# Eight hand-overs in a transformer block kernel: order of the last FFN up products, places and order of the first FFN down tiles, output weights, first values, conv weights, last splits

## The chip, the cores and the metric

The kernel runs on one core of one Trainium2 chip. The metric is the device time of one execution in microseconds (us); lower is better. Times below are of one profiled execution, unless they are called a median of runs.

## The reference, cut to what matters

One block (DEPTH = 1) on a sequence of 1024 rows of 1024 channels, in float32:

```
h = adaLN(rmsnorm(x))
q, k, v, B, C, X, gA, gB = split(h @ w_in)
A   = stick_breaking_attention(q, k, v)        # 16 heads of 64, strictly causal
Bv  = B * causal_dwconv3(C * X)                # short gated convolution
m   = sigmoid(gA) * (A @ w_branch_a) + sigmoid(gB) * (Bv @ w_branch_b)
x   = x + gate1 * (m @ w_out)
h2  = adaLN(rmsnorm(x))
out = x + gate2 * ((silu(h2 @ w_ffn_gate) * (h2 @ w_ffn_up)) @ w_ffn_down)
```

The attention takes, per query block of 128, a sigmoid of the scores, a running product from the diagonal backwards over the keys, and a product with v. In the kernel the running product is a scan on VectorE, and differences of neighbouring v stand in for the product's last factor.

## The kernel before, in words

Every float32 product is done in three: each operand is split into a high half (`whi`, `ath`, `ya[0]`, `rh`: a copy on ScalarE, rounded to the matmul's format) and a low half (`wlo`, `atl`, `ya[1]`, `rl`: the difference, on VectorE), and TensorE adds high x high, high x low and low x high into one PSUM bank. So each weight tile goes: load into a `raw` tile by SyncE's queue, copy on ScalarE, difference on VectorE, matmul. Tiles come from rings: `bufs` of a tag says how many there are, and a new tile waits until the last reader of the tile that had its place has finished.

The stages that the change touches, in order of time:

- *Attention with fillers* (from about 595 to 990 us). `attention()` walks over steps (head, query block of 128): scores `z` (L913, L914), sigmoid on ScalarE into `pt` (L915), scan on VectorE (L923), transposes `tr` (L936), their split `ath`/`atl` (L939, L940), and the product `o` with the values `vt` (L951, L952). `att_load(h)` loads a head's keys, queries and values, `att_dv(h, e)` forms half e of its value differences from the loads `va`, `vb`. Between these, `fillers()` gives TensorE other products: first those of the conv gate with the weights w_cg (L1012 to L1014), later those of branch B. Program order decides TensorE's order here, and the scan's engine follows it; `tc.issue_after(x)` says that what is inside is to be scheduled behind instruction x.
- *Branch A* (about 995 to 1076). The attention output is loaded into `yr` and split into `ya` (L1160 to L1165), then products (m, n) run over m = 0..7 (output tile) and n = 0, 1 (half of the rows) with weights w_a: 24 matmuls each, in the order (0,0), (1,0), (0,1), (1,1), (2,0), (2,1), (3,0) up to (7,1). The result is multiplied by the gate `sgi` (L1184), added to `mb` (L1185) and split into `big` (L1189 on ScalarE, L1190 on VectorE). The bank of a product is one of two. Each weight tile m is a `raw` of 512 KB from the ring `gw` of two (`g_raw`, L505) and four halves. Beside them, `mods_last()` makes the last adaLN sums on VectorE (`ad`, `msum`, L637) and `preload_wo()` loads and splits the first w_out weights w_o (j = 0, 1, 2; L1142 to L1150), called ahead of m = 6. The number behind a name (raw_10551) is its place in the program.
- *Output projection* (from 1076). `ch` is the half of the columns; per row tile i a product with w_o (L1340 to L1342), the gate (`tm`), the residual into `x1`, a store of `x1` and, in the second half, the second norm (`xn`, L1367) and its transposes (L1245).
- *FFN gate and up* as seven-product Strassen steps (`strassen`, products of 12 matmuls at L131 to L133, sums of halves `c` on VectorE at L136, copies of a bank at L1494), ending at about 1594, then *FFN down* (L1590 to L1592) with tiles `f` of the hidden values, which went through memory (`d_f`), and the weights w_d (`wd`).

What sets the order around the change: the five engines and the DMA queues of SyncE, ScalarE and GpSimd each do their instructions in the program's scheduled order, and wait for each other by semaphores.

Of the kernel before, what the change touches and what calls it, by code (L numbers as in the profile page):

```python
# [9 lines left out]
F32 = mybir.dt.float32  # L10
# [7 lines left out]
P = 128  # L18
# [12 lines left out]
def block_kernel(tc, x, x_t, cols, ada_1, ada_2, ada_row, w_q, w_kv, w_cg, w_a, w_b, w_o, w_g, w_u, w_d, out):  # L31
# [94 lines left out]
    def half_prod(ps, w, fh, fl, onto=False):  # L126

        wh = w[0].rearrange("p (k m) -> p k m", k=4)
        wl = w[1].rearrange("p (k m) -> p k m", k=4)
        for k in range(4):  # L130
            nc.tensor.matmul(ps, wh[:, k, :], fh[:, k, :], start=(k == 0 and not onto), stop=False, skip_group_check=onto)  # L131
            nc.tensor.matmul(ps, wh[:, k, :], fl[:, k, :], start=False, stop=False, skip_group_check=onto)  # L132
            nc.tensor.matmul(ps, wl[:, k, :], fh[:, k, :], start=False, stop=(k == 3), skip_group_check=onto)  # L133

# [757 lines left out]
    lastz = [None]  # L892
    lastld = [None]
    npt = [0]
    ats = {}
# [30 lines left out]
    def att_trans(h, i):  # L926
        pt, off = ptof.pop((h, i)), D - (i + 1) * P
        for b0 in range(0, i + 1, 4):
            nb = min(4, i + 1 - b0)
            key = (h, i // 2, b0 // 4)  # L930
            if key not in ats:
                ats[key] = (at_tile("ath"), at_tile("atl")) if ats else first_at
            th, tl = ats[key]
            tr = pps.tile([P, 512], F32, tag="tr", bufs=NTR, name=nm("tr"))
            for j in range(nb):
                nc.tensor.transpose(tr[:, j * P:(j + 1) * P], pt[:, off + (b0 + j) * P:off + (b0 + j + 1) * P], ident)  # L936
            c0 = (i % 2) * P
            src = tr[:, :nb * P].rearrange("p (j t) -> p j t", t=P)
            nc.scalar.activation(th[:, :nb, c0:c0 + P], src, AF.Copy)  # L939
            nc.vector.tensor_tensor(out=tl[:, :nb, c0:c0 + P], in0=src, in1=th[:, :nb, c0:c0 + P].bitcast(F32),  # L940
                                    op=ALU.subtract)
            yield F_T * nb
# [24 lines left out]
    def attention():  # L967

        steps = [(h, i) for h in range(H) for i in (LAST if h == H - 1 else ORDER)]
        for s in range(len(steps) + DAV):  # L970
            flush[0] = s >= len(steps)
            if s < len(steps):
                h, i = steps[s]
                if s % 8 == (0 if h else 3) and h + 1 < H:
                    with tc.issue_after(lastld[0].ins):
                        att_load(h + 1)
                with tc.issue_after(lastz[0].ins) if s else ExitStack():
                    if s in (1, 2):
# [37 lines left out]
    def fillers():  # L1016
        cb_w = {}
        for m, n in [(m + d, n) for m in range(0, KT, 2) for n in range(2) for d in range(2)]:
            if n == 0:
                with tc.issue_after(lastld[0].ins) if m > 1 else ExitStack():  # L1020
                    cb_w[m] = load_ch(w_cg[0, m])
# [13 lines left out]
            nc.sync.dma_start(d_yb[0][n][:, m, :], yh.bitcast(F32))  # L1035
            nc.sync.dma_start(d_yb[1][n][:, m, :], yl.bitcast(F32))
            yield 0.65 * KQ
# [44 lines left out]
    with tc.high_priority():  # L1082
        att_load(0)
        for j in range(HEAD):
            next(fl)
            if j == 1:
                vl = load_vlast(0)
                turn_vlast(0, vl)
                load_v(0, 1)
                load_v(0, 0)  # L1090
                for e in range(2):
                    nc.sync.dma_start((hh, hl)[e][1][:, :4].bitcast(F32), d_h[e])
# [63 lines left out]
    with tc.high_priority():  # L1156
        for n in range(2):
            for k in range(KT):
# [4 lines left out]
                h_, l_ = ya2[:, 0], ya2[:, 1]  # L1163
                nc.scalar.activation(h_, yr, AF.Copy)
                tt(nc.vector, l_, yr, h_.bitcast(F32), ALU.subtract)  # L1165
# [108 lines left out]
    def prod(ps, w, q, onto=False):  # L1274
        half_prod(ps, w, rh[q], rl[q], onto)

# [27 lines left out]
    for ch in range(2):  # L1304
# [21 lines left out]
        for i in (0, 4, 1, 2, 3, 5, 6, 7) if ch else range(8):  # L1326
# [16 lines left out]
            if last:  # L1343
# [4 lines left out]
                pq[2] = product(s00b, 1)  # L1348
            tm = dp.tile([P, 512], F32, tag="tm", bufs=1, name=nm("tm"))
            nc.vector.tensor_tensor(out=tm, in0=ps, in1=g1b[:, cs], op=ALU.mult)  # L1350
            if ch == 0:
                nc.vector.tensor_tensor(out=tm, in0=tm, in1=xi, op=ALU.add)
# [45 lines left out]
    rh[4], rh[5], rl[4], rl[5] = th[:, 4:8], th[:, 0:4], tl[:, 4:8], tl[:, 0:4]  # L1398
    for q in (6, 3):
        rh[q] = ep.tile([P, 4, 512], F32R, name=f"rh{q}")  # L1400
        rl[q] = ep.tile([P, 4, 512], F32R, name=f"rl{q}")
# [69 lines left out]
    def strassen(j, e, src, done=lambda q, c: None):  # L1471
# [11 lines left out]
        else:  # L1483
# [75 lines left out]
    vt = [e2.tile([P, 512], F32, name=f"vt{t}") for t in range(4)]  # L1559
    f0 = e2.tile([P, 2, 512], F32R, tag="f", bufs=6, name=nm("f"))  # L1560
    wd = [bigp.tile([P, 4, 1024], F32, tag="big", bufs=4, name=nm("wd")) for n in range(4)]
    wd = [w_[:, n, :] for w_ in wd for n in range(4)] + [e2.tile([P, 1024], F32, name=nm("wdx")) for n in range(2 * NJ - 16)]
    def get_f(q, j):
        f = e2.tile([P, 2, 512], F32R, tag="f", bufs=6, name=nm("f")) if (q, j) != (0, 0) else f0
        last_f[0] = nc.sync.dma_start(f.rearrange("p a t -> p (a t)").bitcast(F32), d_f[q, j])
        return f
# [196 lines left out]
```

## Time and profile before

| | before |
| --- | --- |
| runs, median (lowest to highest) | 1811.62 us (1808.8 to 1814.61), 3 runs |
| profiled execution | 1812.88 us |
| its span | 1811.1 us, 1.78 us less than its time |
| TensorE busy | 1786.0 us (99%), 8599 matmuls |
| VectorE / ScalarE / GpSimd busy | 1334.5 / 825.2 / 202.2 us |
| mean granted TensorE clock | 0.998 |
| DMA | 359.04 MB, mean 198 GB/s |

How to read it: the span runs from the first to the last instruction; the time has a little around it. A row of a timeline gives start and duration in us, the engine, the line in the code, the operation, what it writes and reads, and in brackets how long the engine had stood idle just before and who released it. Engines: PE is TensorE, DVE is VectorE, ACT is ScalarE, POOL is GpSimd, SP is SyncE, and a q behind the name is its instruction that issues a DMA.

### The profile page before, as it was taken

The numbers are of one execution on the slowest core, as the hardware profiler recorded it, in microseconds if no ns is written. First come the engines' busy times: TensorE is split into PE (matmuls) and PEld (weight loads), VectorE is DVE, ScalarE is ACT, GpSimd is POOL, SyncE is SP. The second block draws the span as 40 slices with busy tenths as digits, with TensorE's granted clock in tenths as the row PEclk, the third lists the DMA queues.
The fourth block names the chain that finished last, engine by engine and source line by source line (L and its number), as shares of the span: only waits on it lengthen the run. The fifth ranks groups of instructions, "written<-read, shape, count | busy, mean of one in ns | idle before, by whom it ended". The sixth has DMA issues, their size and how long they took to land.

```text
span 1811.1 us, 24342 instructions
## 1 busy us (share of the span) xinstructions
PE 1786.0 (99%) x8599; PEld 1485.4 (82%) x8599; DVE 1334.5 (74%) x2030; ACT 825.2 (46%) x1553; POOL 202.2 (11%) x181
## 2 busy tenths in 40 slices
PE   8999999999999999999999999999999999999999
PEld 6888877888888788888887878888888888878887
DVE  6876586787774799999996764698867777644776
ACT  5534364233433567666675221674544444422321
POOL 0024243723231000000000100100000000000000
PEclk9999999999999999999999999999999999999999
DMA  9479654223545977796645866324533444389876
GB/s 383 162 238 392 231 175 140 87 99 115 211 130 175 266 186 195 214 311 180 159 126 175 278 212 214 129 104 157 217 129 144 147 186 162 130 300 338 279 230 223
DMA packets 165006, 359.04 MB, mean 198 GB/s; under 512 B 15539, under 2 KB 60939, under 8 KB 163733
## 3 DMA queue, kind: packets, MB, share of 16 engines
q1 hardware_dynamic: 128300, 289.65, 48.9%
q10 hardware_dynamic: 33096, 55.25, 8.5%
q0 software_dynamic: 3488, 12.59, 2.1%
q8 instruction: 68, 1.11, 0.3%
q14 instruction: 54, 0.43, 0.1%
HBM read 247.84 MB, written 109.62 MB: 197 GB/s over the span
## 4 chain that ended last, share of the span: by engine, by line
PE 84%; DVE 6%; DMA 6%; ACT 3%; issue 2%; SPq 0%; ACTq 0%; POOL 0%; DVEq 0%
PE pj L293 9%; PE e L133 7%; PE e L131 7%; PE e L132 7%; PE pj L133 7%; PE pj L131 7%; PE pj L132 7%; PE e L1590 4%; PE e L1591 4%; PE e L1592 4%; PE tr L936 3%; PE pj L1012 2%; PE pj L1013 2%; PE pj L1014 2%; PE o L952 2%
## 5 line engine op out<-in xcount | busy, mean ns | idle before, releaser
L923 DVE TENSOR_TENSOR_SCAN pt<-pt,mk 128x128 f32<-128x128 f32 (+7 forms) x128 | 172.3, 1346 | 1.5 <-ACT pt L915 1.5
L1221 ACT ACTIVATE whi<-raw 128x512 fp32r<-128x512 f32 x137 | 84.9, 628 | 159.5 <-PE e L132 100.0
L1222 DVE TENSOR_TENSOR wlo<-raw,whi 128x512 fp32r<-128x512 f32 x137 | 93.0, 686 | 68.3 <-ACT whi L1221 50.7
L293 PE MATMUL pj<-whi,big 128*128 128x512 f32 x448 | 133.8, 396 | 3.5 <-ACT big L262 3.5
L132 PE MATMUL e<-big,whi 128*128 128x512 f32 x352 | 136.9, 389 | 0.0
L133 PE MATMUL e<-big,wlo 128*128 128x512 f32 x352 | 136.3, 389 | 0.5 <-DVE wlo L1222 0.5
L131 PE MATMUL e<-big,whi 128*128 128x512 f32 x352 | 136.5, 390 | 0.0
L136 DVE TENSOR_TENSOR c<-pj,c 128x512 f32<-128x512 f32 x140 | 93.2, 681 | 45.1 <-PE pj L133 44.8
L131 PE MATMUL pj<-big,whi 128*128 128x512 f32 x320 | 125.0, 391 | 0.0
L133 PE MATMUL pj<-big,wlo 128*128 128x512 f32 x320 | 124.8, 390 | 0.0
L132 PE MATMUL pj<-big,whi 128*128 128x512 f32 x320 | 124.6, 389 | 0.0
L1590 PE MATMUL e<-whi,f 128*128 128x512 f32 (+1 forms) x319 | 121.7, 382 | 2.5 <-DMA f<-d_f 2.5
L1591 PE MATMUL e<-wlo,f 128*128 128x512 f32 (+1 forms) x319 | 121.8, 382 | 0.0
L1592 PE MATMUL e<-whi,f 128*128 128x512 f32 (+1 forms) x319 | 121.6, 382 | 0.0
L915 ACT ACTIVATE pt<-z,rq 128x512 f32<-128x512 f32 (+1 forms) x192 | 105.2, 576 | 23.6 <-PE z L914 23.2
L1012 PE MATMUL pj<-big,whi 128*128 128x512 f32 x256 | 113.6, 444 | 0.0
L940 DVE TENSOR_TENSOR atl<-tr,ath 128x512 fp32r<-128x512 f32 (+1 forms) x192 | 102.8, 549 | 9.5 <-ACT ath L939 7.6
L939 ACT ACTIVATE ath<-tr 128x512 fp32r<-128x512 f32 (+1 forms) x192 | 93.0, 488 | 29.2 <-PE tr L936 28.2
L131 PE MATMUL e<-rh,whi 128*128 128x512 f32 x264 | 102.8, 389 | 1.4 <-DVE c L136 1.4
L293 PEld LDWEIGHTS pj<-whi,big 128*128 128x128 f32 x448 | 84.9, 190 | 22.0 <-ACT big L262 4.3
L132 PE MATMUL e<-rl,whi 128*128 128x512 f32 x264 | 102.7, 389 | 0.0
L133 PE MATMUL e<-rh,wlo 128*128 128x512 f32 x264 | 102.0, 389 | 0.0
(298 smaller groups left out, 4571.5 us busy)
## 6 DMA issues: line engine op xcount, KB each, us to landing
f<-d_f SPq DMA_DIRECT2D x77, 512.0 KB, 4.6
d_f<-fs SPq DMA_DIRECT2D x70, 512.0 KB, 3.2
raw<-w_cg SPq DMA_DIRECT2D x40, 512.0 KB, 3.8
raw<-w_u SPq DMA_DIRECT2D x26, 512.0 KB, 4.2
raw<-w_g SPq DMA_DIRECT2D x25, 512.0 KB, 4.1
raw<-w_kv SPq DMA_DIRECT2D x20, 512.0 KB, 5.1
ld<-ada SPq DMA_DIRECT2D x16, 512.0 KB, 6.9
d_t<-ts SPq DMA_DIRECT2D x16, 512.0 KB, 6.6
```

Source lines behind the costliest of these rows:

```text
L131: nc.tensor.matmul(ps, wh[:, k, :], fh[:, k, :], start=(k == 0 and not onto), stop=False, skip_group_check=onto)
L132: nc.tensor.matmul(ps, wh[:, k, :], fl[:, k, :], start=False, stop=False, skip_group_check=onto)
L133: nc.tensor.matmul(ps, wl[:, k, :], fh[:, k, :], start=False, stop=(k == 3), skip_group_check=onto)
L136: eng.tensor_tensor(out=out, in0=a, in1=b, op=op)
L293: nc.tensor.matmul(ps, a, b, start=(k == 0 and q == 0), stop=(k == KT - 1 and q == 2))
L915: nc.scalar.activation(pt[:, off + s0:off + s0 + m], z[:, :m], AF.Sigmoid, scale=rq[:, 1, i, h:h + 1])
L923: nc.vector.tensor_tensor_scan(out=pt[:, rev], data0=pt[:, rev], data1=mk[:, rev], initial=1.0, op0=ALU.mult, op1=ALU.max)
L940: nc.vector.tensor_tensor(out=tl[:, :nb, c0:c0 + P], in0=src, in1=th[:, :nb, c0:c0 + P].bitcast(F32), op=ALU.subtract)
L1012: nc.tensor.matmul(ps, wh, rh_, start=(k == 0), stop=False)
L1590: nc.tensor.matmul(o, sh, w[0][:, c], start=(j == 0), stop=False)
L1591: nc.tensor.matmul(o, sh, w[1][:, c], start=False, stop=False)
L1592: nc.tensor.matmul(o, sl, w[0][:, c], start=False, stop=(j == NJ - 1))
```

## The change

Eight edits, each at a place where one engine hands over to another:

1. *First values.* `att_dv(0, 0)` and `att_dv(0, 1)` are made at steps 3 and 4 instead of 1 and 2, and for head 0 the loads of head 1 come after the last store of the first conv tile (`last_yb`) instead of after the last load of head 0.
2. *Conv weights.* The fillers' w_cg loads from m = 2 on come after the loads noted at the end of the head start (`first_ld`) instead of after the latest ones.
3. *Last splits.* ScalarE's halves of `ya` from the eighth on come after the last `ath`.
4. *Output weights.* The raw tiles of w_o j = 1, 2 lie in the ring `gw` that w_a uses; j = 0 keeps its own.
5. *tm.* In the second column half, the gate's multiply writes into `x1` and not into `tm`.
6. *up2.* The split of one up weight comes ahead of the split of a large operand.
7. *Up products.* In the last Strassen step, product p3 is issued after the last matmul of the one ahead of it (`last5`), so behind it.
8. *Down tiles.* Each `f` tile has a place of its own name (f0 to f5), f 4 and 5 are laid first, then two wd tiles, then f 0 to 3; the first seven f are loaded ahead of the wd tiles from 8 on; rh3 is laid ahead of rh6.

```diff
@@ attention
-                    with tc.issue_after(lastld[0].ins):
+                    with tc.issue_after(lastld[0].ins if h else last_yb[0].ins):
                         att_load(h + 1)
-                    if s in (1, 2):
-                        att_dv(0, s - 1)
+                    if s in (3, 4):
+                        att_dv(0, s - 3)
@@ fillers
-                with tc.issue_after(lastld[0].ins) if m > 1 else ExitStack():
+                with tc.issue_after(first_ld.ins) if m > 1 else ExitStack():
                     cb_w[m] = load_ch(w_cg[0, m])
@@ preload_wo
-            raw = wx.tile([P, 1024], F32, tag="raw", bufs=1, name=nm("raw"))
+            raw = (gw if j else wx).tile([P, 1024], F32, tag="raw", bufs=GR if j else 1, name=nm("raw"))
@@ ya
-                nc.scalar.activation(h_, yr, AF.Copy)
+                with tc.issue_after(last_ath[0].ins) if n * KT + k > 6 else ExitStack():
+                    nc.scalar.activation(h_, yr, AF.Copy)
@@ output projection
             x1 = dp.tile([P, D], F32, tag="x1", bufs=2, name=nm("x1"))
             nc.scalar.dma_start(x1[:, :512], d_x1[i, :, :512])
-            nc.vector.tensor_tensor(out=x1[:, cs], in0=tm, in1=xi, op=ALU.add)
+            nc.vector.tensor_tensor(out=x1[:, cs], in0=ps, in1=g1b[:, cs], op=ALU.mult)
+            nc.vector.tensor_tensor(out=x1[:, cs], in0=x1[:, cs], in1=xi, op=ALU.add)
@@ FFN
+    up2 = split(ws1[1])
     split_big(rh[4], rl[4], h2b[0][1])
-    up2 = split(ws1[1])
...
-            prod(p1, split(s1), 4, True)
+            last5 = prod(p1, split(s1), 4, True)
...
-        p3 = product(sp_4 or split(s4), 2)
+        with tc.issue_after(last5.ins) if (j, e) == (NJ - 1, 1) else ExitStack():
+            p3 = product(sp_4 or split(s4), 2)
@@ down
+    fring = {n: f_tile(n) for n in (4, 5)}
+    wdx = [e2.tile([P, 1024], F32, name=nm("wdx")) for n in range(2)]
+    fring.update((n, f_tile(n)) for n in range(4))
...
+    for ht in range(7):
+        ftiles[0, ht] = get_f(0, ht)
+        if ht == 1:
+            f1_ld = last_f[0]
     for ht in range(NJ):
-        load_wd(ht, 0)
-        if ht < 7:
-            ftiles[0, ht] = get_f(0, ht)
+        with tc.issue_after(f1_ld.ins) if ht > 7 else ExitStack():
+            load_wd(ht, 0)
```

How this moves instructions. SyncE, branch A. The loads raw_10551 and raw_10627 are w_a m = 6 and 7; raw_10525, raw_10535 and raw_10545 are w_o j = 0, 1, 2; sgi and mb belong to the products (3,1) to (4,1) here. Before:

```order
451 L1181 DMA mb_10311<-d_mb 128x512
452 L1179 DMA sgi_10267<-d_sga 128x512
453 L505 DMA raw_10551<-w_a 128x1024
454 L1181 DMA mb_10360<-d_mb 128x512
455 L1179 DMA sgi_10309<-d_sga 128x512
456 L1181 DMA mb_10396<-d_mb 128x512
457 L1179 DMA sgi_10358<-d_sga 128x512
458 L505 DMA raw_10627<-w_a 128x1024
```

And now, at the same place, and later, where sgi_10594 is the gate tile of (6,1), which waits until its ring's tile of (5,1) has been read for the last time:

```order
450 L1184 DMA sgi_10221<-d_sga 128x512
451 L1148 DMA raw_10535<-w_o 128x1024
452 L1186 DMA mb_10311<-d_mb 128x512
453 L1186 DMA mb_10360<-d_mb 128x512
454 L1184 DMA sgi_10267<-d_sga 128x512
455 L1184 DMA sgi_10309<-d_sga 128x512
456 L1186 DMA mb_10396<-d_mb 128x512
457 L1148 DMA raw_10545<-w_o 128x512
```

```order
467 L1184 DMA sgi_10561<-d_sga 128x512
468 L1184 DMA sgi_10594<-d_sga 128x512
469 L1148 DMA raw_10525<-w_o 128x1024
470 L506 DMA raw_10551<-w_a 128x1024
471 L506 DMA raw_10627<-w_a 128x1024
```

The loads of w_o j = 1, 2 stand where those of w_a m = 6, 7 stood, and these have moved behind w_o j = 0; before, all three w_o loads stood behind them, in rows 471, 473 and 474.

VectorE, from the multiply of product (5,1) (sgi_10479) to that of (6,0) (sgi_10561); wlo of raw_10551 and raw_10627 are the low halves of w_a m = 6, 7. Before, and now:

```order
1202 L1184 TENSOR_TENSOR sgi_10479<-pj_10483,sgi_10479 128x512
1203 L637 ISA ad_10512,msum_10304<-ad_10512,cab_10045 128x1024
1204 L637 ISA msum_10304 128x1
1205 L136 TENSOR_TENSOR wlo_10634<-raw_10627,whi_10633 128x512
1206 L1185 TENSOR_TENSOR sgi_10479<-sgi_10479,mb_10481 128x512
1207 L136 TENSOR_TENSOR msum_10304<-msum_10304,cst 128x8
1208 L1190 TENSOR_TENSOR big_10130<-sgi_10479,big_10129 128x512
1209 L1184 TENSOR_TENSOR sgi_10561<-pj_10565,sgi_10561 128x512
```

```order
1202 L137 TENSOR_TENSOR msum_10304<-msum_10304,cst 128x8
1203 L1195 TENSOR_TENSOR big_10130<-sgi_10479,big_10129 128x512
1204 L1153 TENSOR_TENSOR wlo_10528<-raw_10525,whi_10527 128x512
1205 L1153 TENSOR_TENSOR wlo_10532<-raw_10525,whi_10531 128x512
1206 L1153 TENSOR_TENSOR wlo_10538<-raw_10535,whi_10537 128x512
1207 L1153 TENSOR_TENSOR wlo_10542<-raw_10535,whi_10541 128x512
1208 L1153 TENSOR_TENSOR wlo_10548<-raw_10545,whi_10547 128x512
1209 L137 TENSOR_TENSOR wlo_10554<-raw_10551,whi_10553 128x512
1210 L137 TENSOR_TENSOR wlo_10558<-raw_10551,whi_10557 128x512
1211 L137 TENSOR_TENSOR wlo_10630<-raw_10627,whi_10629 128x512
1212 L137 TENSOR_TENSOR wlo_10634<-raw_10627,whi_10633 128x512
1213 L1189 TENSOR_TENSOR sgi_10561<-pj_10565,sgi_10561 128x512
```

Five differences of w_o and all four of w_a m = 6, 7 now stand between the last step of (5,1) (big_10130) and the multiply of (6,0). The load of raw_10551 takes the place of raw_10535, so it waits for the difference in row 1207. The load of raw_10627 waits for the one in row 1208.

VectorE at the weights of m = 4 (raw_10348): sgi_10185 is the multiply of (2,0), sgi_10221 that of (2,1). Before, and now:

```order
1153 L1184 TENSOR_TENSOR sgi_10185<-pj_10189,sgi_10185 128x512
1154 L637 ISA ad_10218,msum_10091<-ad_10218,cab_10045 128x1024
1155 L637 ISA msum_10091 128x1
1156 L1185 TENSOR_TENSOR sgi_10185<-sgi_10185,mb_10187 128x512
1157 L136 TENSOR_TENSOR wlo_10351<-raw_10348,whi_10350 128x512
```

```order
1150 L1195 TENSOR_TENSOR big_10130<-sgi_10098,big_10129 128x512
1151 L1195 TENSOR_TENSOR big_10130<-sgi_10136,big_10129 128x512
1152 L137 TENSOR_TENSOR wlo_10351<-raw_10348,whi_10350 128x512
1153 L137 TENSOR_TENSOR wlo_10355<-raw_10348,whi_10354 128x512
1154 L1189 TENSOR_TENSOR sgi_10185<-pj_10189,sgi_10185 128x512
1155 L638 ISA ad_10218,msum_10091<-ad_10218,cab_10045 128x1024
```

Both differences of m = 4 have moved ahead of the multiply of (2,0). They write into the tiles of m = 2, so the second of them waits for the last matmul of (2,1).

More of the change, by code (lines that the diff above doesn't have):

```diff
@@ L132, in half_prod @@
             nc.tensor.matmul(ps, wh[:, k, :], fl[:, k, :], start=False, stop=False, skip_group_check=onto)
-            nc.tensor.matmul(ps, wl[:, k, :], fh[:, k, :], start=False, stop=(k == 3), skip_group_check=onto)
+            last = nc.tensor.matmul(ps, wl[:, k, :], fh[:, k, :], start=False, stop=(k == 3), skip_group_check=onto)
+        return last
     def tt(eng, out, a, b, op):
@@ L893, in block_kernel @@
     lastld = [None]
+    last_yb = [None]
+    last_ath = [None]
     npt = [0]
@@ L938, in att_trans @@
             src = tr[:, :nb * P].rearrange("p (j t) -> p j t", t=P)
-            nc.scalar.activation(th[:, :nb, c0:c0 + P], src, AF.Copy)
+            last_ath[0] = nc.scalar.activation(th[:, :nb, c0:c0 + P], src, AF.Copy)
             nc.vector.tensor_tensor(out=tl[:, :nb, c0:c0 + P], in0=src, in1=th[:, :nb, c0:c0 + P].bitcast(F32),
@@ L1035, in fillers @@
             nc.sync.dma_start(d_yb[0][n][:, m, :], yh.bitcast(F32))
-            nc.sync.dma_start(d_yb[1][n][:, m, :], yl.bitcast(F32))
+            last_yb[0] = nc.sync.dma_start(d_yb[1][n][:, m, :], yl.bitcast(F32))
             yield 0.65 * KQ
@@ L1090, in block_kernel @@
                 load_v(0, 0)
+                first_ld = lastld[0]
                 for e in range(2):
@@ L1274, in prod @@
     def prod(ps, w, q, onto=False):
-        half_prod(ps, w, rh[q], rl[q], onto)
+        return half_prod(ps, w, rh[q], rl[q], onto)
     def product(w, q):
@@ L1348, in block_kernel @@
                 pq[2] = product(s00b, 1)
-            tm = dp.tile([P, 512], F32, tag="tm", bufs=1, name=nm("tm"))
-            nc.vector.tensor_tensor(out=tm, in0=ps, in1=g1b[:, cs], op=ALU.mult)
             if ch == 0:
+                tm = dp.tile([P, 512], F32, tag="tm", bufs=1, name=nm("tm"))
+                nc.vector.tensor_tensor(out=tm, in0=ps, in1=g1b[:, cs], op=ALU.mult)
                 nc.vector.tensor_tensor(out=tm, in0=tm, in1=xi, op=ALU.add)
@@ L1398, in block_kernel @@
     rh[4], rh[5], rl[4], rl[5] = th[:, 4:8], th[:, 0:4], tl[:, 4:8], tl[:, 0:4]
-    for q in (6, 3):
+    for q in (3, 6):
         rh[q] = ep.tile([P, 4, 512], F32R, name=f"rh{q}")
@@ L1559, in block_kernel, with f_tile @@
     vt = [e2.tile([P, 512], F32, name=f"vt{t}") for t in range(4)]
-    f0 = e2.tile([P, 2, 512], F32R, tag="f", bufs=6, name=nm("f"))
+    def f_tile(n):
+        return e2.tile([P, 2, 512], F32R, tag=f"f{n % 6}", bufs=1, name=nm("f"))
+    fring = {n: f_tile(n) for n in (4, 5)}
+    wdx = [e2.tile([P, 1024], F32, name=nm("wdx")) for n in range(2)]
+    fring.update((n, f_tile(n)) for n in range(4))
+    nf = itertools.count()
     wd = [bigp.tile([P, 4, 1024], F32, tag="big", bufs=4, name=nm("wd")) for n in range(4)]
-    wd = [w_[:, n, :] for w_ in wd for n in range(4)] + [e2.tile([P, 1024], F32, name=nm("wdx")) for n in range(2 * NJ - 16)]
+    wd = [w_[:, n, :] for w_ in wd for n in range(4)] + wdx
+    wd += [e2.tile([P, 1024], F32, name=nm("wdx")) for n in range(2 * NJ - 18)]
     def get_f(q, j):
-        f = e2.tile([P, 2, 512], F32R, tag="f", bufs=6, name=nm("f")) if (q, j) != (0, 0) else f0
+        n = next(nf)
+        f = fring.pop(n) if n in fring else f_tile(n)
         last_f[0] = nc.sync.dma_start(f.rearrange("p a t -> p (a t)").bitcast(F32), d_f[q, j])
```

## The prediction

> **What bounds the kernel now.** I read the profile's page first: busy time, then the chain that ended last. The first row below gives each engine's busy time and share of the span, the second the chain's shares.
>
> ```profile
> PE 1786.0 (99%) x8599; PEld 1485.4 (82%) x8599; DVE 1334.5 (74%) x2030; ACT 825.2 (46%) x1553; POOL 202.2 (11%) x181
> PE 84%; DVE 6%; DMA 6%; ACT 3%; issue 2%; SPq 0%; ACTq 0%; POOL 0%; DVEq 0%
> ```
>
> TensorE is busy 1786.0 of 1811.1 us. No change of order can win more than the 25 us that are left, and any new wait of TensorE lengthens the kernel by its whole length. So the second view is the list of what TensorE waits for (total, times, longest, us); its largest rows that the change can reach:
>
> ```profile
> PE tr L936 <- DVE pt L923: 4.3, 9, 1.8
> PE e L1590 <- DMA f<-d_f: 2.5, 1, 2.5
> PE o L951 <- ACT ath L939: 2.4, 2, 1.3
> ```
>
> The third view, TensorE's timeline, gives each a place (start, duration, and in brackets the idle time ahead of it):
>
> ```profile
> 603.18 0.44 PE L936 MATMUL tr<-dm,pt 128*128 128x128 f32 x2 [1.80 <-DVE pt L923]
> 666.74 0.39 PE L951 MATMUL o<-ath,vt 128*128 128x256 f32 x1 [1.05 <-ACT ath L939]
> 667.47 0.39 PE L952 MATMUL o<-atl,vt 128*128 128x256 f32 x1 [0.34 <-DVE atl L940]
> 986.16 0.39 PE L951 MATMUL o<-ath,vt 128*128 128x256 f32 x1 [1.35 <-ACT ath L939]
> 987.60 0.39 PE L952 MATMUL o<-atl,vt 128*128 128x256 f32 x1 [0.36 <-DVE atl L940]
> 1082.63 0.50 PE L1340 MATMUL e<-whi,big 128*128 128x512 f32 x1 [1.28 <-ACT whi L1148]
> 1138.58 1.09 PE L1245 MATMUL e<-dm,xn 128*128 128x128 f32 x8 [0.78 <-ACT xn L1367]
> 1198.73 0.50 PE L133 MATMUL e<-big,wlo 128*128 128x512 f32 x1 [0.54 <-DVE wlo L1222]
> 1591.66 0.50 PE L131 MATMUL e<-rh,whi 128*128 128x512 f32 x1 [1.41 <-DVE c L136]
> 1597.19 0.47 PE L1590 MATMUL e<-whi,f 128*128 128x512 f32 x1 [2.51 <-DMA f<-d_f]
> ```
>
> These are the places of the eight hand-overs. All brackets together are 1.80 + 1.39 + 1.71 + 1.28 + 0.78 + 0.54 + 1.41 + 2.51 = 11.42 us: the most that the change can take away here.
>
> **The change part by part: what it takes away.** Behind three of the brackets stands another engine's wait for a load. ScalarE's two and SyncE's issue, and the time from issue to landing of such a load (the last figure of the last row):
>
> ```profile
> 664.99 0.63 ACT L516 ACTIVATE whi<-raw 128x512 fp32r<-128x512 f32 x1 [3.14 <-DMA raw<-w_cg]
> 984.99 0.63 ACT L1164 ACTIVATE ya<-yr 128x512 fp32r<-128x512 f32 x1 [5.95 <-DMA yr<-d_ya]
> 1591.38 5.79 SPq L1565 DMA_DIRECT2D f<-d_f  x6
> f<-d_f SPq DMA_DIRECT2D x77, 512.0 KB, 4.6
> ```
>
> *Conv weights* (1.39 us): ScalarE stood 3.14 us at a w_cg split with ath behind it; its load now goes out after an earlier one, so it has landed. *Last splits* (1.71 us): ScalarE stood 5.95 us at a ya split, ath behind it; the last nine splits now come after the last ath. They then follow each other through a ring of two yr tiles, and cost up to 2 us if the branch-A products overtake them. *Output weights* (1.28 us): the third w_o load left only when the branch-A products had ended; now it leaves far ahead. *tm* (0.78 us): the multiply writes into x1 and no longer waits until tm has been stored; if x1's ring of two had no tile free, the wait would stay. *up2* (0.54 us): the split that TensorE waited for moves ahead of a larger one, which comes one split later, itself used later. *Up products* (1.41 us): twelve matmuls of another product, 12 x 0.227 = 2.72 us (the pitch comes below), now lie between the copy and the product that needs the sum, and cover 1.41. *Down tiles* (2.51 us): the f loads were issued from 1591.38, behind wd loads, when the up products were nearly over; in the new order the first four need only a product that ends 48 matmuls, or 10.9 us, before the last, and such a load takes 4.6 us. I take all seven whole: 1.39 + 1.71 + 1.28 + 0.78 + 0.54 + 1.41 + 2.51 = 9.62 us.
>
> *First values* I set at nothing. VectorE waited for a load of vb, while scans stood behind:
>
> ```profile
> 601.83 0.69 DVE L136 TENSOR_TENSOR vb<-vb,va 128x512 f32<-128x512 f32 x1 [2.60 <-DMA vb<-d_v]
> 602.44 0.68 DVE L923 TENSOR_TENSOR_SCAN pt<-pt,mk 128x256 f32<-128x256 f32 x1
> 606.17 0.28 PE L951 MATMUL o<-ath,vt 128*128 128x256 f32 x1
> ```
>
> Now the scan goes first and TensorE's 1.80 us go. But the first `o` needs vt, and vt now stands behind that scan and eight more VectorE instructions: from about 600.4 on some 7 us of work on VectorE by the durations of such rows, so it comes at 606.5 to 607.4, as late as the 606.17 of before. The wait moves from the transpose to `o`. Bounds: 1.80 us won (and up to 1 us of small waits behind it) to 1.5 us lost, if the next head's loads, which now leave later, are late too. I take 0, as the rows give no net either way.
>
> **What it adds: w_a behind w_o.** This is the large term. The raw tiles of w_o j = 1, 2 now lie in the ring of two that w_a uses, and are allotted ahead of w_a m = 6, 7. So the load of w_a m = 6 waits until w_o j = 1 has been split. Its splits stand on ScalarE and VectorE behind those of w_o j = 0; and the load of j = 0 stands on SyncE behind a sgi load that waits for the last step of product (5,1). After (5,1) TensorE has only (6,0), which needs w_a m = 6. So from the end of (5,1) on everything runs in series. I price it by the same steps in the trace of before, where they ran after (6,1):
>
> ```profile
> 1054.28 0.39 PE L1012 MATMUL pj<-ya,whi 128*128 128x512 f32 x1
> 1065.32 0.39 PE L1012 MATMUL pj<-ya,whi 128*128 128x512 f32 x1
> 1065.52 0.69 DVE L1184 TENSOR_TENSOR sgi<-pj,sgi 128x512 f32<-128x512 f32 x1 [1.38 <-PE pj L1014]
> 1057.61 1.22 DVE L637 CUSTOM_DVE_ANT_0 ad<-ad,cab 128x1024 f32<-128x1024 f32 x1
> 1067.63 0.69 DVE L1190 TENSOR_TENSOR big<-sgi,big 128x512 fp32r<-128x512 f32 x1 [0.70 <-ACT big L1189]
> 1068.35 0.32 SPq L1179 DMA_DIRECT2D sgi<-d_sga  x1
> 1064.53 0.42 SPq L1144 DMA_DIRECT2D raw<-w_o  x1
> 1069.08 1.15 ACT L1148 ACTIVATE whi<-raw 128x512 fp32r<-128x512 f32 x2 [1.48 <-DMA raw<-w_o]
> 1069.75 1.29 DVE L1149 TENSOR_TENSOR wlo<-raw,whi 128x512 fp32r<-128x512 f32 x2 [1.43 <-ACT whi L1148]
> 1056.27 0.61 ACT L516 ACTIVATE whi<-raw 128x512 fp32r<-128x512 f32 x1
> ```
>
> (6,0) starts at 1054.28 without a gap after (5,1), and (7,0) at 1065.32: 48 matmuls and one small transpose in 11.04 us, so a pitch of about 0.227 when some 0.15 is given to the transpose. Now the chain. From the end of (6,1), 1065.32, to the sgi load, 1068.35, are 3.03 us; plus 0.37 until the next issue (the row's 0.32 and 0.05). Behind (5,1) an `ad` stands between the multiply and the add: 1.0 more (its 1.22, of which 0.2 overlaps its neighbours). Sum 4.40. The w_o load of 512 KB: 1064.53 to 1069.08, 4.55. Four splits in place of two: 0.67 from the ScalarE start to VectorE's, 1.29 for two, 1.2 for two more: 3.16. The load of w_a m = 6, of the same size: 4.55, with 0.05 to issue it. Its first split on ScalarE: 0.63. Together 4.40 + 4.55 + 3.16 + 0.05 + 4.55 + 0.63 = 17.34 us in which TensorE stands. Nothing covers it: the one transpose of msum is its only other work.
>
> The Trainium skill, page "DMA: Bandwidth & Descriptors", section "Anatomy of one DMA", fits 2.0 us plus bytes over 436 GB/s for a GpSimd-issued transfer: as an estimate 3.2 us for 512 KB. By it the chain would be 14.6 us and the forecast 2.7 us lower. The row of this very load on SyncE's queue says 4.55 and decides.
>
> **A cold start.** The trace has one wait of more than 3 us, at the beginning: the timeline rows give it, and the windows give the granted clock (the last three figures are clock, DMA share, GB/s).
>
> ```profile
> 10.31 2.93 PE L293 MATMUL pj<-whi,big 128*128 128x512 f32 x6 [3.51 <-ACT big L262]
> 15.60 2.07 PE L293 MATMUL pj<-whi,big 128*128 128x512 f32 x8
> 10.00:15.00 5.00, 4.69 (x11) 3.72 (x12) 4.93 (x10) 2.73 (x5) 0.00 (x0) 0.50 1.01 379
> 15.00:20.00 5.00, 5.00 (x22) 4.06 (x21) 4.96 (x10) 3.72 (x6) 0.00 (x0) 0.92 1.02 419
> ```
>
> After 3.51 us of rest the clock was 0.50 for 5 us: twelve matmuls took 15.60 - 10.31 = 5.29 us, at the full pitch 2.72. After 17 us of rest I expect the same at (6,0): 2.57 us more. The Trainium skill, page "TensorE: Matmul & The Clock Gate", section "Part 1: The HAM clock gate", speaks against the change here: it says that TensorE's clock is halved after an idle window of about 3.4 us and comes back after as long a busy one. The trace agrees with the half clock; by the page's window the loss would be 1.7 us as an estimate, and the sum 0.9 us lower.
>
> *Two smaller waits.* VectorE's order puts both w_a m = 4 low halves ahead of the multiply of (2,0). The second needs its tiles free, so (2,1) finished; and (3,0) needs the bank which that multiply frees. TensorE waits for ScalarE 0.61 + VectorE 0.69 + 0.69 = 2.0 us (bounds 1 to 2.5). And (0,1) and (1,1) now run interleaved, so the multiply of (0,1) is hardly begun when (2,0) wants its bank: one multiply of 0.69 less two matmuls, about 0.5 (0 to 0.7).
>
> **The sum.** -9.62 + 0 + 17.34 + 2.57 + 2.0 + 0.5 = +12.8 us. The profiled execution took 1812.88 us, its span 1811.1 and 1.8 around it; it is 1.3 above the median of the runs, 1811.62. So 1825.7 by its own time and 1824.4 by the median: I say 1825.
>
> **The rivals.** *TensorE is not held at (6,0)*: faster. If w_o j = 0 were loaded and split while (5,1) runs, w_a m = 6 would land in time. For it: in the trace of before w_a's loads run far ahead of use, and SyncE is hardly busy. Against it: the order of SyncE puts w_o j = 0 behind the sgi load of (6,1), which waits for the last step of (5,1). Time: 1812.88 - 9.62 + 2.5 = 1805.8. It decides from where the wait at (6,0), the cold start counted, falls below 9.62 - 2.5 = 7.1 us: then nothing is lost. *One landing in place of two*: w_o j = 0 is there in time, but its splits still come behind the multiply of (5,1), and w_a m = 6 behind them: 0.2 + 0.6 + 3.2 + 4.6 + 0.63 = 9.2 us and the cold start: 1812.88 - 9.62 + 9.2 + 2.57 + 2.5 = 1817.5, about the edge of what can be told. For it speaks only that the place of j = 0 might be free earlier. *The change doesn't do what it says at the down tiles and up products*: the f loads stay behind wd, or the wait moves to the wd splits; 3.9 us not won, 1829.6. Against it: the places of f 0 to 3 are another tile's now.
>
> **How the numbers follow.** A measurement of this kernel tells about 0.3% from no change, 5.4 us: 1806.2 to 1817.1. Forecast 0.75 (slower throughout), down tiles without effect 0.08 (slower), one landing 0.09 (half slower, half within), TensorE not held 0.08 (faster two in three, else within). Slower 0.75 + 0.08 + 0.045 = 0.875, within 0.045 + 0.027 = 0.07, faster 0.053; for errors in the seven gains taken whole I move 0.02: slower 0.85, within 0.09, faster 0.06. For the range, the landings of the loads of w_a (and others on their line) and of w_o in the trace, least, median and most:
>
> ```profile
> DMA to landing us min/median/max: 3.1/4.2/7.7
> DMA to landing us min/median/max: 5.5/5.5/5.5
> ```
>
> Low end: two landings of 3.1 us (14.4 for the chain), half the clock's cost, the first values' gain, 1 us at (3,0): 1816 on the median's scale, and I say 1815. High end: landings of 5.5 us (19.2), the first values' loss, two gains missing: about 1831.
>
> **What would show it.** In the changed profile: TensorE idle 14 to 19 us ahead of (6,0), from about 1054 on, the waits list led by a `pj` on the whi of w_a; a granted clock near 0.5 in the 5 us behind; SyncE's w_o load right behind a sgi load, and w_a's about 8 us behind that; a wait of 2 us ahead of (3,0); the brackets of the seven gains gone; in the first head a wait of `o` on vt. A gap under 7 us ahead of (6,0) proves the sum wrong; so does a full clock behind it, by 2.6 us.

## The result, and the profile after

The changed kernel takes 1834.81 us (median of 4 runs, 1833.4 to 1837.07), the kernel before 1811.88 us (median of 4, 1808.8 to 1814.61). The ratio is 1.0125, 95% interval 1.0107 to 1.0143: 23 us slower. The forecast was 1825 us, 13 us slower, with a range up to 1831: the way was right, the size was not. The profiled execution of the changed kernel has a span of 1832.4 us, 21.3 us longer than before.

From its page, busy time and the shares of the chain that ended last; then the largest rows of what TensorE waits for (total, times, longest, us; the two rows left out, of 2.9 and 2.5 us, lie in the first 11 us of the kernel, and the kernel before has them too, with 3.5 and 2.5):

```profile
PE 1789.6 (98%) x8599; PEld 1489.5 (81%) x8599; DVE 1333.7 (73%) x2030; ACT 827.8 (45%) x1553; POOL 200.7 (11%) x181
PE 90%; DVE 4%; DMA 4%; issue 1%; ACT 1%; SPq 0%; DVEq 0%; ACTq 0%
```

```profile
PE pj L1015 <- ACT whi L517: 12.2, 1, 12.2
PE pj L1015 <- DVE sgi L1189: 6.7, 3, 3.3
PE tr L648 <- DVE msum L137: 5.5, 1, 5.5
PE tr L939 <- DVE pt L926: 3.1, 7, 1.0
...
PE o L954 <- DVE vt L137: 2.5, 1, 2.5
...
PE pj L1015 <- ACT ya L1169: 2.3, 1, 2.3
```

None of the seven waits that were to go is in this list; every new wait of over 0.6 us is in branch A or in the first head. TensorE's timeline gives the places (the first row is the first `o`; the others are the interleaved (0,1) and (1,1), which the expectations below call (1,0), then (2,0), (3,0), (5,0), the msum transpose behind (5,1), and (6,0)):

```profile
607.40 0.58 PE L954 MATMUL o<-ath,vt 128*128 128x256 f32 x1 [2.53 <-DVE vt L137]
1008.22 0.73 PE L1015 MATMUL pj<-ya,whi 128*128 128x512 f32 x2 [2.30 <-ACT ya L1169]
1010.45 0.50 PE L1015 MATMUL pj<-ya,whi 128*128 128x512 f32 x1 [0.32 <-DVE sgi L1189]
1024.95 0.77 PE L1015 MATMUL pj<-ya,whi 128*128 128x512 f32 x1 [3.33 <-DVE sgi L1189]
1052.74 0.47 PE L1015 MATMUL pj<-ya,whi 128*128 128x512 f32 x1 [3.08 <-DVE sgi L1189]
1069.35 0.45 PE L648 MATMUL tr<-dm,msum 128*128 128x128 f32 x1 [5.46 <-DVE msum L137]
1082.00 0.79 PE L1015 MATMUL pj<-ya,whi 128*128 128x512 f32 x1 [12.20 <-ACT whi L517]
```

Ahead of (6,0) TensorE stood 5.46 + 12.20 = 17.66 us, where 17.34 were forecast. The chain is the one that the forecast described, in its order, in the rows of VectorE, SyncE and ScalarE:

```profile
1062.60 0.69 DVE L1189 TENSOR_TENSOR sgi<-pj,sgi 128x512 f32<-128x512 f32 x1 [4.51 <-DMA sgi<-d_sga]
...
1066.10 0.68 DVE L1189 TENSOR_TENSOR sgi<-pj,sgi 128x512 f32<-128x512 f32 x1
1070.31 0.42 SPq L1148 DMA_DIRECT2D raw<-w_o  x1
1074.75 2.71 ACT L1152 ACTIVATE whi<-raw 128x512 fp32r<-128x512 f32 x5 [4.65 <-DMA raw<-w_o]
1077.94 0.93 SPq L506 DMA_DIRECT2D raw<-w_a  x2
1081.32 1.15 ACT L517 ACTIVATE whi<-raw 128x512 fp32r<-128x512 f32 x2 [3.86 <-DMA raw<-w_a]
```

The w_o load takes 1074.75 - 1070.31 = 4.44 us (4.55 forecast), the splits 1077.94 - 1074.75 = 3.19 (3.16), the w_a load 1081.32 - 1077.94 = 3.38 (4.60). What is longer is the beginning: the multiply of (5,1) starts at 1066.10, over 2 us behind the product's last matmul, which starts at 1063.50, since that of (5,0) had waited 4.51 us for its gate tile (first row). That delay is no part of the forecast chain. (5,0) waited for a multiply that stood in the same way, and (3,0) did so for a part of its wait.

So the unforeseen part lies in branch A ahead of (6,0): 2.30 + 0.32 + 3.33 + 3.08 = 9.03 us of waits, against 2.5 in the sum.

### The profile page after: what moved, and what is told of

It is laid out like the page before. It is cut to its first block, busy times and chain, and to the rows that moved or that the text cites. A ratio compares the mean times of both kernels' runs of the same rounds, so it can differ in the third digit from the quotient of the medians.

```text
span 1832.4 us, 24338 instructions
## 1 busy us (share of the span) xinstructions
PE 1789.6 (98%) x8599; PEld 1489.5 (81%) x8599; DVE 1333.7 (73%) x2030; ACT 827.8 (45%) x1553; POOL 200.7 (11%) x181
## 4 chain that ended last, share of the span: by engine, by line
PE 90%; DVE 4%; DMA 4%; issue 1%; ACT 1%; SPq 0%; DVEq 0%; ACTq 0%
PE e L132 8%; PE e L133 8%; PE e L131 8%; PE pj L131 7%; PE pj L133 7%; PE pj L132 7%; PE pj L294 7%; PE e L1610 4%; PE e L1612 4%; PE e L1611 4%; PE pj L1015 3%; PE pj L1016 3%; PE pj L1017 3%; PE tr L939 3%; PE o L955 2%; PE z L916 2%
## 5 line engine op out<-in xcount | busy, mean ns | idle before, releaser
L1226 ACT ACTIVATE whi<-raw 128x512 fp32r<-128x512 f32 x137 | 84.9, 628 | 161.6 <-PE e L132 101.5
L1227 DVE TENSOR_TENSOR wlo<-raw,whi 128x512 fp32r<-128x512 f32 x137 | 93.1, 687 | 70.7 <-ACT whi L1226 53.3
L137 DVE TENSOR_TENSOR wlo<-raw,whi 128x512 fp32r<-128x512 f32 x108 | 80.8, 753 | 35.1 <-ACT whi L517 35.0
L517 ACT ACTIVATE whi<-raw 128x512 fp32r<-128x512 f32 x108 | 67.0, 627 | 84.7 <-PE pj L132 47.1
```

The costliest lines, as they stand in the source:

```text
L137: eng.tensor_tensor(out=out, in0=a, in1=b, op=op)
```

## The experiments

Two theories could tell where these 9 us come from: the w_o loads, which took w_a's place in SyncE's queue, or the last splits. The edit with the w_o loads alone is this:

```diff
-            raw = wx.tile([P, 1024], F32, tag="raw", bufs=1, name=nm("raw"))
+            raw = (gw if j else wx).tile([P, 1024], F32, tag="raw", bufs=GR if j else 1, name=nm("raw"))
```

> The kernel before with the output-weights edit alone (raw tiles of w_o j = 1, 2 in w_a's ring). Theory A (the loss of the change is the sum of two separate ones, output weights and last splits): TensorE waits 17 to 18 us ahead of (6,0) and restarts for some 1.5 us at half clock, the wait of 1.28 us at the first w_o products goes, nothing else changes: 1811.9 + 17.7 + 1.5 - 1.3 = 1829.8 us. Theory B (the waits ahead of (1,0), (3,0) and (5,0) that the changed profile shows also come from the w_o loads, which took their place in SyncE's queue): these 9 us and a second restart at half clock come with it, about 1841 us.

Measured: 1830.35 us beside 1814.21 for the kernel before, ratio 1.0092 (1.0071 to 1.0113). The waits of branch A:

```profile
PE pj L1012 <- ACT whi L516: 12.8, 1, 12.8
...
PE tr L647 <- DVE msum L136: 3.1, 1, 3.1
```

15.9 us ahead of (6,0), and no wait on a gate tile or on ya. The list keeps its 2.5 us at the down tiles and 1.4 at the up products. Theory A holds here: output weights cost about 16 us by themselves.

The last splits alone:

```diff
-                nc.scalar.activation(h_, yr, AF.Copy)
+                with tc.issue_after(last_ath[0].ins) if n * KT + k > 6 else ExitStack():
+                    nc.scalar.activation(h_, yr, AF.Copy)
```

> The kernel before with the last-splits edit alone (ScalarE's ya halves from the eighth on behind the last ath). Theory A: the waits of the changed profile ahead of (1,0), (3,0) and (5,0), 2.3 + 0.3 + 3.3 + 3.1 us, and 2.4 us of half clock behind the second, belong to this edit; the 1.7 us at the last heads go: 1811.9 + 11.4 - 1.7 = 1821.6 us. Theory B: they belong to the w_o loads, so only the gain is left: 1810.2 us.

Measured: 1825.8 us, ratio 1.007 (1.0053 to 1.0088), so 9 to 16 us slower; theory B's 1810 is out. Its waits:

```profile
PE pj L1013 <- DVE sgi L1186: 5.2, 2, 3.2
...
PE pj L1013 <- ACT ya L1166: 2.2, 1, 2.2
PE e L1342 <- ACT whi L1223: 2.1, 1, 2.1
```

The first two are the waits of branch A that the changed kernel has (the 5.2 us are 1.97 ahead of (3,0) and 3.25 ahead of (5,0)); the third, at the output projection, it has not. In its span, 1822.2 us, 11.1 above before's, half clock has a share as well, at three of these waits and once more at the down tiles, which the edit doesn't touch.

The first values alone:

```diff
-                    with tc.issue_after(lastld[0].ins):
+                    with tc.issue_after(lastld[0].ins if h else last_yb[0].ins):
                         att_load(h + 1)
...
-                    if s in (1, 2):
-                        att_dv(0, s - 1)
+                    if s in (3, 4):
+                        att_dv(0, s - 3)
```

> The kernel before with the first-values edit alone. From the changed profile: waits of 0.99, 2.53 and 0.30 us in the first head and 0.9 us of half clock in place of 1.80 + 0.18 + 0.22 + 0.37 + 0.29 us: about 1.9 us slower, 1813.8 us. My term in the prediction, a mere exchange, would be 1811.9 us.

Measured: 1815.49 us, ratio 1.001 (0.9999 to 1.002): within what can be told from no change. Both waits of the trade are there: `o` waits for vt, and a score product of the second head for its keys `skl` (the last run below tells which half of the edit makes which):

```profile
PE o L952 <- DVE vt L136: 2.5, 1, 2.5
...
PE z L915 <- DMA skl<-d_k: 2.2, 1, 2.2
```

The five edits that are left, in the changed kernel without the three above:

> The changed kernel without output weights, last splits and first values: conv weights, tm, up2, up products and down tiles are left. If each takes away its whole wait, 1.39 + 0.78 + 0.54 + 1.41 + 2.51 = 6.6 us: 1805.3 us. If waits taken away early come back later as others, 1808 to 1812 us.

Measured: 1803.54 us, ratio 0.9949 (0.9933 to 0.9966), 6 to 12 us faster; the span is 1803.8, 7.3 us below before's. The largest rows at places that the change touches are waits that these five edits don't reach:

```profile
PE tr L939 <- DVE pt L926: 5.0, 9, 2.2
...
PE o L954 <- ACT ath L942: 2.0, 1, 2.0
...
PE e L1344 <- ACT whi L1152: 0.6, 1, 0.6
```

The waits at conv weights, tm, up2, up products and down tiles are gone, and no new one of over 0.6 us has come; two old ones are longer, at the first transpose (2.2 us for 1.8) and at the last heads (2.0 for 1.35). The four ratios less one add up to 0.92 + 0.70 + 0.10 - 0.51 = 1.21%, against 1.25% for the whole change. With intervals of 0.1 to 0.2% either way on each, that says no more than that the parts nearly add up.

Next, what in each of the two costly edits does it. For output weights, one thing is moved and all eight edits stay:

```diff
+        if n == 0 and m not in wa:
+            wa[m] = load_ch(w_a[m])
         if (m, n) == (KT - 2, 0):
+            wa[m + 1] = load_ch(w_a[m + 1])
             for _ in ml:
                 pass
...
                 preload_wo()
-        if n == 0:
-            wa[m] = load_ch(w_a[m])
```

> The changed kernel with one thing moved: the raw tiles of w_a m = 6, 7 are allotted ahead of those of w_o j = 1, 2 in the ring that they share; all eight edits stay. Theory: the 17.7 us ahead of (6,0) and the 1.5 us of half clock behind them come from the order in the ring alone, and the 1.3 us gain at the first w_o products stays: 1834.8 - 19.2 = 1815.6 us. Rival: the load of w_o j = 0, which still goes out late behind a sgi load, is the real cause, and TensorE then waits for it ahead of the first w_o products, some 5 us and more: 1821 us or above.

Measured: 1815.17 us, ratio 1.0015 (1.0006 to 1.0024), with nothing left of the wait ahead of (6,0) nor of one at the first w_o products:

```profile
PE pj L1015 <- DVE sgi L1190: 5.8, 2, 3.1
PE tr L939 <- DVE pt L926: 2.7, 7, 0.9
PE o L954 <- DVE vt L137: 2.5, 1, 2.5
...
PE pj L1015 <- ACT ya L1169: 2.0, 1, 2.0
```

The edit moves the whole call that allots, loads and splits a w_a tile. That the splits stand behind w_o's in the program is no loss by itself: the kernel before is written so too, with a ring of its own for w_o, and has no wait there. So it takes both, the shared ring and w_o's place ahead of w_a in it. The late load of w_o j = 0 costs nothing as long as w_a is not behind it.

For the last splits, VectorE's order shows what happened. Its steps from the multiply of (3,0) on, with the edit alone (`sgi<-pj` is a multiply, `sgi<-sgi` the add, `big` the last step; ad, msum and wlo left out):

```
sgi_10267<-pj_10271   sgi_10267<-sgi_10267,mb_10269   sgi_10309<-pj_10313
sgi_10309<-sgi_10309,mb_10311   big_10042<-sgi_10267   big_10130<-sgi_10309
sgi_10358<-pj_10362   sgi_10358<-sgi_10358,mb_10360   sgi_10394<-pj_10398
```

The multiply of (3,1) (sgi_10309) comes ahead of the last step of (3,0) (big_10042). There are two gate tiles. The tile of (3,0) is read for the last time in `big`, and only then may the gate of (4,0) be loaded. In the changed kernel that looks so (SyncE and VectorE; the multiply is that of (4,0)):

```profile
1043.64 2.07 SPq L1184 DMA_DIRECT2D sgi<-d_sga  x2
...
1051.91 0.69 DVE L1189 TENSOR_TENSOR sgi<-pj,sgi 128x512 f32<-128x512 f32 x1 [6.55 <-DMA sgi<-d_sga]
```

And in the kernel before (the two multiplies are those of (4,0) and (4,1), the two loads the gates of (4,1) and (5,0)):

```profile
1041.79 0.68 DVE L1184 TENSOR_TENSOR sgi<-pj,sgi 128x512 f32<-128x512 f32 x1
1041.90 0.32 SPq L1179 DMA_DIRECT2D sgi<-d_sga  x1
1045.64 0.32 SPq L1179 DMA_DIRECT2D sgi<-d_sga  x1
...
1047.78 0.69 DVE L1184 TENSOR_TENSOR sgi<-pj,sgi 128x512 f32<-128x512 f32 x1 [2.17 <-DMA sgi<-d_sga]
```

Before, the gates were loaded one by one, 4 to 7 us apart. That of (4,0) went out at 1035.42, 6.4 us ahead of its multiply, which didn't wait for it; the multiply of (4,1) waited 2.17 us for its own, which the second bank hid. Now the two are loaded as a pair, that of (4,0) only when TensorE is about done with the product, and VectorE waits 6.55 us, more than the bank hides: (5,0) stood 3.08 us. With the edit kept and only this order pinned:

```diff
-        last_m = nc.vector.tensor_tensor(out=sa, in0=ps, in1=sa, op=ALU.mult)
+        with tc.issue_after(last_lo.ins) if it else ExitStack():
+            last_m = nc.vector.tensor_tensor(out=sa, in0=ps, in1=sa, op=ALU.mult)
...
-        nc.vector.tensor_tensor(out=mlo[n][:, m, :], in0=sa, in1=mh[n][:, m, :].bitcast(F32), op=ALU.subtract)
+        last_lo = nc.vector.tensor_tensor(out=mlo[n][:, m, :], in0=sa, in1=mh[n][:, m, :].bitcast(F32), op=ALU.subtract)
```

> The kernel before with the last-splits edit and one order pinned: on VectorE the multiply of a branch-A product comes after the last step of the product ahead of it, as in the kernel before. Theory: with that edit alone the scheduler put the steps of two products side by side, so the ring of two gate tiles is loaded in pairs and late, and the multiply waits for its load; pinned, the waits ahead of (3,0) and (5,0) (2.0 and 3.2 us) and their half clock (some 1.6 us) go, the ya wait of 2.2 us stays: 1825.8 - 6.8 = 1819 us, less if a half clock elsewhere in that run doesn't come back. Rival: the gate loads are late because the ya loads crowd the DMA engines, whatever the order: 1825 us.

Measured: 1814.11 us, ratio 1.0007 (0.9998 to 1.0016); the gates go out one by one again (those of (4,0), (4,1) and (5,0) at 1034.64, 1040.48 and 1044.22), no wait of TensorE on a gate tile is left, and the ya wait is:

```profile
PE pj L1013 <- ACT ya L1166: 2.7, 1, 2.7
```

It came out 5 us lower than expected: the 2.1 us at the output projection and the half clock there and at the down tiles, which the run of the edit alone had, are gone too. The order on VectorE, which the edit moved through the scheduler, made most of the loss (0.70% without the pin, 0.07% with it). That the ya loads crowd the DMA engines was not the cause: the edit that delays the ya splits is still in this run.

Both put right, with all eight edits:

> All eight edits, with only two orders put right: w_a m = 6, 7 allotted ahead of w_o j = 1, 2, and VectorE's multiply of a branch-A product behind the last step of the one ahead of it. Theory (each of the two orders is worth what it was alone): of the run with the first put right (1815.2 us) the two waits on a gate tile, 2.7 + 3.1 us, and the half clock behind them, some 3 us, go: 1806.4 us; the ya wait of 2 to 2.7 us, the vt wait of 2.5 and the skl wait of 1.8 stay. Rival: the two waits move to another step of branch A once it runs sooner: 1811 us or above.

Measured: 1807.55 us, ratio 0.9974 (0.9965 to 0.9984). The gate waits have fallen to 0.3 us, and what is left of the eight edits' own cost is in the first head and in ya:

```profile
PE o L954 <- DVE vt L137: 2.5, 1, 2.5
...
PE pj L1015 <- ACT ya L1169: 2.3, 1, 2.3
PE z L917 <- DMA skl<-d_k: 1.6, 1, 1.6
```

A version that takes the gains without these: w_a ahead of w_o, the order pinned, the first values as before, and only the tenth and eleventh ya split behind the last ath (`n * KT + k in (9, 10)`):

> Seven edits, two of them mended: w_a m = 6, 7 allotted ahead of w_o j = 1, 2; only the tenth and eleventh ya split behind the last ath, VectorE's order pinned; first values as before. Against the run of the five others (1803.5 us): 0.6 us at the first w_o products and 2.4 us at the last heads go: 1800.5 us. Rival: the tenth and eleventh split still bring a wait of branch A for ya or for a gate tile, so 1803 to 1806 us.

Measured: 1801.15 us, ratio 0.9933 (0.9918 to 0.9948), the lowest median with the next, as expected; the interval overlaps that of the five others (0.9933 to 0.9966), so it isn't shown to be faster than they are. Branch A waits once for 0.3 us. Then the first values, at steps 2 and 3:

> The same with the first values at steps 2 and 3 in place of 1 and 2, the loads of the second head as before. VectorE's order then is scan, vb, atl, scan, vt: the scan no longer waits for vb, and vt has only three instructions more ahead of it. Theory: of the 2.2 us at the first transpose and the 2 us of smaller waits behind it some 2 us go: 1798.5 us. Rival: vt is late again, as in the run of first values alone, and o waits as long: 1800.5 us.

Measured: 1801.38 us, ratio 0.9933 (0.9917 to 0.995): no difference. The wait at the first transpose fell to 0.23 us, but waits of 0.39, 0.53 and 1.10 us follow in the same head; the theory's 2 us didn't come. Its 2.2 us at the first transpose were taken from the profile of the five others; in the mended kernel's own profile that wait was 1.16 us. And half of the first-values edit alone, on the kernel before:

```diff
-                    if s in (1, 2):
-                        att_dv(0, s - 1)
+                    if s in (3, 4):
+                        att_dv(0, s - 3)
```

> The kernel before with half of the first-values edit: the values at steps 3 and 4, the second head's loads where they were. Theory: the wait of o on vt, 2.5 us in the run of the whole edit, comes from VectorE's order; with the cy and ybl steps no longer ahead of vt it is 1 to 2 us; the skl wait of 2.2 us and its 1.3 us of half clock, which come from the late loads, go: 1810 us. Rival: the order alone makes both waits: 1813.5 us, as the whole edit.

Measured: 1812.11 us beside 1812.49, ratio 0.9997 (0.9986 to 1.0007). The skl wait is gone, so it came from the late loads; `o` still waits for vt, 1.8 us:

```profile
PE o L951 <- DVE vt L136: 1.8, 1, 1.8
```

## Why the prediction was wrong in size

Point by point, in the order of its steps.

- *The seven gains, 9.62 us.* Right within the interval. Five of them together measure 0.51% (0.34 to 0.67), so 6 to 12 us, for 6.63; the waits at the first w_o products and the last heads are gone too, but the edit of the last heads paid more for it than it won.
- *First values, 0.* Right within what can be told: 1.001 (0.9999 to 1.002). The wait did move from the transpose to `o` on vt. That the next head's loads would be late too was the bound of that term, and it came: 2.2 us in the edit's own run, 0.3 in the changed kernel. In the changed profile the first head has waits of 0.99 + 2.53 + 0.30 = 3.82 us for 1.80 + 0.18 + 0.22 + 0.37 + 0.29 = 2.86 before, and from 608 to 611 us a granted clock of 0.53, some 1.4 us more.
- *w_a behind w_o, 17.34.* Right, in its mechanism and its size: 17.66 in the changed kernel, 15.9 alone. This term decided the sign. That the size fits so closely is partly luck: in the changed kernel the beginning was about 2.2 us longer than in the sum (the late gate of (5,0)), and the w_a load 1.2 us shorter.
- *Cold start, 2.57.* It came, but smaller: behind 1082.00 about 1.6 us. In the window below, TensorE starts 15 matmuls in its 5.0 busy us, which at the pitch of 0.227 are 3.4. The 1.7 us that the prediction gave beside its own figure were nearer.
- *(3,0), 2.0, and (2,0), 0.5.* (2,0) measures 0.32. (3,0) measures 3.33 and 2.6 us of half clock behind it (15 matmuls in 6.05 busy us). The low halves of w_a m = 4 did stand ahead of the multiply, and in the run of the last splits alone, where that multiply waits for no gate, (3,0) stands 1.97 us, as forecast. In the changed kernel the step was wrong in what ends last: behind the low halves VectorE waited 1.27 us more, for the gate's load.

```profile
1024.11 0.69 DVE L1189 TENSOR_TENSOR sgi<-pj,sgi 128x512 f32<-128x512 f32 x1 [1.27 <-DMA sgi<-d_sga]
```

- *Last splits, -1.71 with "up to 2 us if the branch-A products overtake them".* This is the step that failed. They did overtake: 2.30 us, since the last yr load, issued at 1001.33, was split at 1007.53, 6.2 us later. And I priced the edit by what it moves on ScalarE alone. What it moved on VectorE, two products' steps side by side, I had read in the order only at (2,0); that the ring of gate tiles is then loaded in pairs and late, I didn't price at all. (5,0) was no term of the sum, nor the half clock at (3,0). In the changed profile the waits of branch A ahead of (6,0) are 9.0 us and the half clock behind them 2.6, and the edit wins 1.7, so 9.9, where my sum had 0.8 for it (2.0 + 0.5 - 1.71). These 9 us are most of the 10 that are missing between the forecast and 1834.8. Of the 9.0 us, 7.4 are in the edit's own run too; the other 1.6 (the 1.27 of the gate ahead of (3,0), and (2,0)) show only in kernels with more of the edits. Its own run says 0.70% (0.53 to 0.88), 9.6 to 15.9 us.

The half clock (a granted clock near 0.5, at which TensorE starts a matmul every 0.43 us in place of every 0.227) is the part that no sum of waits shows. Five windows, each from just ahead of a wait's end; the count behind TensorE's busy time is its matmuls, and the third figure from the right is the granted clock. The changed kernel behind (6,0), after 12.20 us of rest, and behind (3,0), after 3.33; then the first down products in three kernels: before, after 2.51 us of rest; the last splits alone, after 2.32; first values alone, after 2.44:

```profile
1081.00:1087.00 6.00, 5.00 (x15) 4.02 (x16) 2.58 (x4) 2.30 (x4) 0.00 (x0) 0.65 0.17 67
```

```profile
1024.90:1031.00 6.10, 6.05 (x15) 4.78 (x16) 5.28 (x9) 1.23 (x2) 1.05 (x2) 0.53 0.67 195
```

```profile
1596.00:1602.00 6.00, 4.81 (x21) 4.02 (x22) 5.30 (x10) 0.74 (x2) 0.53 (x1) 1.00 0.95 339
```

```profile
1606.00:1612.00 6.00, 5.35 (x17) 4.25 (x18) 5.30 (x10) 1.10 (x2) 0.53 (x1) 0.72 1.00 325
```

```profile
1597.00:1603.00 6.00, 5.30 (x16) 4.25 (x17) 5.30 (x10) 1.15 (x2) 0.53 (x1) 0.72 0.97 334
```

## What to carry to other kernels

When a tile joins a ring that another stream uses, ask whose load waits for its last reader, and walk that chain back to the engine's queue: an allotment written earlier in the program is a dependency. When an edit shifts a scheduled order, list what moved on every engine that shares a ring with it, and for each ring ask when the last reader of a tile now comes and how long the load behind it takes; a wait of 2 us that a second bank hides becomes visible when the load leaves a few us later. And take edits apart before judging a bundle: five of these eight were worth 0.5%, and two orders put right turned 1.25% slower into 0.26% faster with all eight.

## What the runs showed of the hardware

- *Half clock after short rests, and not always.* At the same place in three kernels, 2.51 us of rest left the clock at 1.00, and 2.32 and 2.44 us brought a mean of 0.72 over 6 us (17 and 16 matmuls in 5.3 busy us, where 23 would fit). The Trainium skill, page "TensorE: Matmul & The Clock Gate", section "Part 1: The HAM clock gate", gives one idle window of about 3.4 us as the condition and says that the window runs free of the kernel. By that rule none of the three should have slowed down; two did, so the measurement decides that shorter rests can be enough. That the same rest sometimes costs and sometimes doesn't agrees with a free-running window, but no run here shows the window itself. Shorter ones still were followed by it: at the last heads, rests of 1.36 and 0.34 us in the run with half of first values left the clock at 0.50 from 988 to 990, and 1.49 and 0.36 in output weights alone at 0.69 from 989 to 992, where 1.35 and 0.36 in the kernel before did not; and 3.08 us ahead of (5,0) in the changed kernel did not either (1.00 from 1052.7 to 1058). So a stretch of half clock in one profile of an edit need not be the edit's.
- *A small load can be slow, and a large one varies.* The gate tiles of 256 KB took 2.6 to 7.6 us from issue to landing in the changed kernel (the row below: least, median, most); in the rows further above, the gate of (4,0) was issued 8.3 us ahead of the multiply that waited for it. The w_a load of 512 KB took 3.4 us with the DMA engines 68% busy (the last figure but one of the second row), where the w_o load of the same size had taken 4.55 in the kernel before with them 62% busy (third row). In these two, the share of busy DMA engines did not tell how long the load takes.

```profile
DMA to landing us min/median/max: 2.6/4.8/7.6
```

```profile
1078.00:1081.30 3.30, 0.00 (x0) 0.00 (x0) 0.51 (x1) 0.00 (x0) 0.00 (x0) 0.50 0.68 230
```

```profile
1064.50:1069.00 4.50, 4.50 (x22) 3.72 (x21) 2.08 (x3) 0.63 (x1) 0.00 (x0) 1.00 0.62 213
```

What stays open: why the first head doesn't gain from scans that no longer wait. Three orders of its values gave 1.001, 0.9997 and, in the mended kernel, no difference, with the waits each time at other instructions of the same head. Single profiles can't tell it: the longest wait at a first transpose is 1.16 us in the mended kernel, 1.80 in the kernel before, 2.24 in the five others and 2.96 in output weights alone, all of them with the values at their old place.
